# The second mixer's identity and ones move among its first constants, and its state sums move to other PSUM banks

## The chip, the core and the metric

The kernel runs on one core of a Trainium2 chip. The metric is the time of one execution on the device in microseconds (us); lower is better. A core has a matrix engine (TensorE, PE in the profile, with its weight loads as PEld), a vector engine (VectorE, DVE), a scalar engine (ScalarE, ACT), a general engine (GpSimd, POOL) and an engine that in this kernel issues nearly all transfers (SyncE, SP). Each engine runs its instructions in order and waits for semaphores that other engines or transfers raise.

## The reference, cut to what matters

One layer of a hybrid decoder runs for a prompt of 2048 tokens and for a sample group of 8 sequences with 8 tokens each (64 tokens), with the same weights:

```python
proj = x @ w_in                      # columns of mixers A, B and C
oa, delta_new = gated_delta_chunked(...)          # mixer A, chunks of 64
ob, lru_new   = rg_lru(...)                       # mixer B
oc, gla_new   = gla_chunked(qc, kc, vc, logf, s0) # mixer C, 6 heads, dk=32, dv=64
oc = head_rms_norm(oc, norm_c_w) * jax.nn.silu(zc)
heads = concatenate([oa, ob, oc])
x = layer_norm(ALPHA * x + heads @ w_out, ln1_g, ln1_b)
x = layer_norm(ALPHA * x + conv_ffn(x), ln2_g, ln2_b)
```

Mixer C in one chunk, with state S per sequence and head, and decay f = exp(logf):

```python
b = cumsum(logf); b_last = b[-1]
o     = (q * exp(b)) @ S + (att(q, k, b)) @ v
S_new = exp(b_last) * S + (k * exp(b_last - b)).T @ v
```

The prompt starts from S = 0; the sample group starts from 8 given states (s_gla), and its 8 new states are outputs.

## The kernel before

The program has four parts in a row. `phase1` makes the combined projection. `window_a` runs mixer A (`deltanet`), with a projection of the gates (`gates`) as dense filling. `window_c` runs mixer C (`Gla`) together with the output projection and the first LayerNorm (`Project`). `phase3` is the FFN; its order is written by hand. In `window_a` and `window_c` the order of the instructions on every engine, the SP queue included, is worked out when the program is built, by a planner that simulates the time line with estimated costs; program order counts as priority, and a block under `high_priority` with a negative number comes later than that.

Memory: a pool of tiles lies behind the pool made before it, and a window's pools take the addresses of the window before. A tile can be written as soon as the last reader of what lay there is done. In `window_c` the pools are, in this order: ce and cf (early tiles), c1 and c2, then those of `Project` (o1, o2, o3 with the LayerNorm rows l1g and l1b), and last c3, with the identity and the ones. The early pools lie where mixer A's early tiles were, c3 at the end, where mixer A's last working tiles were.

Mixer C works on nine groups: the sample group (number 8) first, then eight groups of 256 prompt tokens. `load` fetches b (cumulated decay), k, q and v; v has one buffer. `prep` of a group is `natural` (decay factors, on DVE and ACT), `tokens` and, for each of six heads, `fill` (builds the score operands on ACT, POOL and by transfers K<-KN) and `scores` (matmuls s, L1373). `tokens` transposes v (pv, L1394) and the decayed k (pk, L1399) on PE against the identity and copies the results on ACT into XC (L1395) and KC (L1400); for the sample group these are XCs and KCs. RC, XC and KC are rings of two for the prompt's groups.

`sample` loads the 8 states into four spare tiles of the projection (spmx, spmh, spml, spxt; two states each, L1446), makes the outputs (po, L1451 and L1453), normalizes them, and after a `yield` makes the new states: a masked copy of v (L1458), the old state times its decay (L1460), and for each of the 8 states six matmuls into a PSUM bank (ss, L1466), added on DVE (L1467) and stored (L1468). That second half is resumed when group 0 has been prepared. `chain` takes a group's four chunks in turn: new state (cs, L1427), output (po, L1430), copy of the state (L1436), and after two chunks the norm (`head_norm`).

`Project.weights` loads the eight pieces of w_out (wos, 512 KB each, through three buffers that the residual rows x share) and splits each into a high part on ACT (woh, L1495) and a low part on DVE or POOL (wol, L1496). `Project.__call__`, at low priority, multiplies 128 tokens by them (pm, L320, two tiles of 48 matmuls in all), adds the residual (L1531) and normalizes; `transposed` turns the result for the FFN (pt, L1549).

PSUM: eight banks of 2 KB per partition. Mixer C's scores have two (tag s), the transpositions one (tk), po two, cs one; the projection's pool has two (tag pm). The eight sums ss use the tag cs.

`head_norm` ends mixer A too: its last output is stored (s_mix<-ob, L986), and then the tiles it used are free.

Of the kernel before, what the change touches and what calls it, by code (L numbers as in the profile page):

```python
# [8 lines left out]
F32 = mybir.dt.float32  # L9
# [294 lines left out]
def load_consts(E, pool, names):  # L304
    t = {}
    for n in names:
        o, w = _CST[n]
        t[n] = pool.tile([128, w], F32, name="c_" + n)
        E.nc.sync.dma_start(t[n], E.d["consts"][:, o:o + w])
    return t  # L310
# [397 lines left out]
def deltanet(E, ctx, pools, need, ahead):  # L708
# [341 lines left out]
    for gs in pairs:  # L1050
        for g in gs:
            prep(g)
        inverse(gs)
        ahead(gs[0].pair)
        for g in gs:
            blocks(g)
        last = gs[-1].smp
        for g in (gs[0], *gs[2:], gs[1]):
            tokens(g)
            weights(g)  # L1060
            if g.b == 7:
                with tc.high_priority(-100):
                    sample()
            if not g.smp:
                chain(g)
# [147 lines left out]
class Gla:  # L1213
# [4 lines left out]
    def __init__(self, E, ctx):  # L1218
        nc, tc = E.nc, E.tc
        self.E = E  # L1220
        E.aset(LNEXP)
        early = ctx.enter_context(tc.tile_pool(name="ce", bufs=1))
        self.early = ctx.enter_context(tc.tile_pool(name="cf", bufs=2))
        pool = ctx.enter_context(tc.tile_pool(name="c1", bufs=1))
        self.tr = ctx.enter_context(tc.tile_pool(name="c2", bufs=2))
        self.pg = {t: ctx.enter_context(tc.tile_pool(name="c" + t, bufs=1, space=PSUM)) for t in ("s", "tk", "g")}
        self.C = load_consts(E, early, ["m2", "m3", "m2s", "bj", "i32"])

        def ring(name, n, c, w):
            return [pool.tile([128, 6, c, w], F32, name=f"{name}{i}") for i in range(n)]  # L1230

        self.RC, self.XC, self.KC = ring("RC", 2, 4, 64), ring("XC", 2, 4, 64), ring("KC", 2, 4, 32)
        sg = [early.tile([128, 6, 1, 64], F32, name="RCs")], ring("XCs", 1, 1, 64), ring("KCs", 1, 1, 32)
        self.slots = [{n: early.tile([128, 256], F32, name=f"{n}_{i}") for n in ("K1", "Q1", "K2", "Q2", "K3", "Q3")}
                      for i in range(2)]
        self.sls = [{n: early.tile([128, 64], F32, name=f"{n}_s{i}") for n in ("K2", "Q2")} for i in range(2)]

        self.KN = [{l: early.tile([128, 512 >> t], F32, name=f"KN{l}_{t}") for l in (1, 2, 3)} for t in range(2)]

        self.DD = [{l: early.tile([128, n, 6], F32, name=f"D{l}_{i}") for l, n in ((1, 4), (2, 16), (3, 64))}  # L1240
                   for i in range(2)]
        self.ebs = pool.tile([32, 6, 8], F32, name="ebs")
        for r in sg:
            nc.vector.memset(r[0][0:64], 0.0)
        nc.vector.memset(sg[0][0][64:], 0.0)
        for d in self.sls + self.KN + self.slots:
            for w in d.values():
                nc.gpsimd.memset(w, 0.0)
        for d in self.DD:
            for w in d.values():  # L1250
                nc.gpsimd.memset(w, 1.0)
        for w in self.RC + self.XC + self.KC:
            nc.gpsimd.memset(w[0:64], 0.0)
        self.G = []
        for g in range(9):
            o = Env()
            o.g, o.smp, o.t0 = g, g == 8, g * 256
            o.RC, o.XC, o.KC = (r[0] for r in sg) if o.smp else (r[g % 2] for r in (self.RC, self.XC, self.KC))
            o.nch = 1 if o.smp else 4
            o.n = 64 * o.nch  # L1260
            self.G.append(o)
# [177 lines left out]
            if c % 2 == 1:  # L1439
                self.norm(po, z, g.t0 + 64 * (c - 1))  # L1440

    def sample(self, g, room):
        nc, E, C = self.E.nc, self.E, self.C
        S0 = big = room
        for i in range(4):
            nc.sync.dma_start(S0[i][0:32], E.d["s_gla"][:, 2 * i:2 * i + 2])  # L1446
        po, z = self.outputs(g.t0)
        for h in range(6):
            p, h2 = divmod(h, 2)
            o = po[h2 * 64:(h2 + 1) * 64, p]  # L1450
            nc.tensor.matmul(o, g.XC[64:, h, 0], g.RC[64:, h, 0], start=True, stop=False)  # L1451
            for b in range(8):
                nc.tensor.matmul(o[:, b * 8:(b + 1) * 8], S0[b // 2][0:32, b % 2, h],  # L1453
                                 g.RC[0:32, h, 0, b * 8:(b + 1) * 8], start=False, stop=b == 7)
        self.norm(po, z, g.t0)
        yield
        for i in range(4):
            nc.vector.tensor_tensor(big[i][64:], g.XC[64:, None, :, 0].to_broadcast([64, 2, 6, 64]),  # L1458
                                    C["bj"][64:, 2 * i:2 * i + 2, None, None].to_broadcast([64, 2, 6, 64]), op=OP.mult)
            nc.vector.tensor_tensor(S0[i][0:32], S0[i][0:32],  # L1460
                                    self.ebs[:, :, 2 * i:2 * i + 2, None].rearrange("p h b o -> p b h o")
                                    .to_broadcast([32, 2, 6, 64]), op=OP.mult)
            for b in range(2):
                ps = self.psum(f"ss{i}{b}", (32, 6, 64), "cs", 1)
                for h in range(6):
                    nc.tensor.matmul(ps[:, h], g.KC[64:, h, 0], big[i][64:, b, h], start=True, stop=True)  # L1466
                nc.vector.tensor_tensor(S0[i][0:32, b], S0[i][0:32, b], ps, op=OP.add)  # L1467
            nc.sync.dma_start(E.d["o_glas"][:, 2 * i:2 * i + 2], S0[i][0:32])  # L1468
        yield
# [85 lines left out]
def window_c(E):  # L1555

    with ExitStack() as ctx:
        C = Gla(E, ctx)
        P = Project(E, ctx)
        C.C.update(load_consts(E, ctx.enter_context(E.tc.tile_pool(name="c3", bufs=1)), ["ident", "ones"]))  # L1560
        room = P.spare()
        C.dest = P.dest
        order = [C.G[8]] + C.G[:8]
        C.load(order[0])
        for i, g in enumerate(order):
            if i < 8:
                C.load(order[i + 1])
            C.prep(g)
            if g.smp:
                smp = C.sample(g, room)  # L1570
                next(smp)
                P.weights()
            else:
                if g.g == 0:
                    next(smp)
                C.chain(g)
            for t0 in range(g.t0, g.t0 + g.n, 128):
                with E.tc.high_priority(-10 ** 5):
                    P(t0)
                    P.transposed(C.C["ident"], 1)  # L1580
        P.transposed(C.C["ident"])
# [373 lines left out]
def program(tc, dram):  # L1955

    E = Env()
    E.nc, E.tc, E.d = tc.nc, tc, dram
    with ExitStack() as ctx:
        setup(E, ctx)  # L1960
        phase1(E)
        window_a(E)
        window_c(E)
        phase3(E)
# [16 lines left out]
```

## Time and profile before

| | us |
|---|---|
| median of 3 runs | 3026.18 |
| lowest and highest | 3017.28, 3026.94 |
| the profiled execution | 3025.96 |
| its span, first to last instruction | 3024.2 |
| PE busy in the span | 2886.8 |
| DVE, ACT, POOL busy | 1510.9, 1231.4, 844.2 |

Mixer A and the gates run from about 540 to 1037 us of the span, mixer C and the output projection from about 982 to 1525, and the FFN behind that. Times in the rows are us from the start of the span, mean times in ns where the column says so. A row of a stretch gives its bounds, its length, and then for PE, PEld, DVE, ACT and POOL the busy time and, in brackets, the number of instructions; behind them stand the granted clock of PE (1.00 is full), the share of the DMA engines and GB/s. Where a stretch is asked for one line only, only engines that run this line are shown. In a row of a line or tile the three numbers are least, median and greatest duration in ns, and then come the starts of the first and the last instruction. A row of waits reads: who waited, for whom, us in total, times, longest.

### The profile page before, as it was taken

The numbers are of one execution on the slowest core, as the hardware profiler recorded it, in microseconds if no ns is written. First come the engines' busy times: TensorE is split into PE (matmuls) and PEld (weight loads), VectorE is DVE, ScalarE is ACT, GpSimd is POOL, SyncE is SP. The second block draws the span as 40 slices with busy tenths as digits, with TensorE's granted clock in tenths as the row PEclk, the third lists the DMA queues.
The fourth block names the chain that finished last, engine by engine and source line by source line (L and its number), as shares of the span: only waits on it lengthen the run. The fifth ranks groups of instructions, "written<-read, shape, count | busy, mean of one in ns | idle before, by whom it ended". The sixth has DMA issues, their size and how long they took to land.

```text
span 3024.2 us, 45238 instructions
## 1 busy us (share of the span) xinstructions
PE 2886.8 (95%) x17755; PEld 2490.4 (82%) x17755; DVE 1510.9 (50%) x2454; ACT 1231.4 (41%) x2591; POOL 844.2 (28%) x898
## 2 busy tenths in 40 slices
PE   8999999788889799999899999999999999999998
PEld 7888789777779577767678888888889999999997
DVE  4564443577663676756533333333376443344436
ACT  4474443446653687766332222222232222222223
POOL 0000001734423545444222222222232222222224
PEclk9999999789999579999899999999999999999999
DMA  6221113533433443533531111111134111111111
GB/s 198 83 74 68 58 59 96 144 101 111 114 95 99 108 130 110 150 112 117 180 116 45 46 56 49 51 48 42 49 112 146 42 52 47 48 42 42 49 43 62
DMA packets 196508, 256.77 MB, mean 85 GB/s; under 512 B 43170, under 2 KB 162040, under 8 KB 196232
## 3 DMA queue, kind: packets, MB, share of 16 engines
q1 hardware_dynamic: 194168, 246.58, 26.6%
q0 software_dynamic: 1984, 7.12, 0.6%
q8 instruction: 140, 2.29, 0.3%
q14 instruction: 72, 0.59, 0.1%
q10 hardware_dynamic: 144, 0.20, 0.0%
HBM read 183.94 MB, written 60.08 MB: 81 GB/s over the span
## 4 chain that ended last, share of the span: by engine, by line
PE 60%; DVE 4%; ACT 2%; DMA 1%; issue 1%; POOL 1%; SPq 0%; DVEq 0%; POOLq 0%; ACTq 0%
PE pug L320 16%; PE pd L320 15%; PE puv L320 15%; PE pm L320 6%; PE s L1373 2%; DVE y L1788 1%; PE pd L1870 1%; PE cs L1427 1%; ACT Q L1360 1%; PE zp L1121 1%; PE po L1206 0%; PE zp L1122 0%; PE po L1430 0%; PE zp L1123 0%; DVE act L1724 0%
## 5 line engine op out<-in xcount | busy, mean ns | idle before, releaser
L1724 DVE SCALAR_TENSOR_TENSOR act<-G,cols,act 128x1024 f32<-128x1024 f32 (+1 forms) x132 | 123.6, 950 | 492.0 <-ACT act L1722 489.6
L1877 DVE TENSOR_TENSOR y<-y,pd 128x512 f32<-128x512 f32 x322 | 220.9, 687 | 203.2 <-PE pd L320 196.7
L1615 POOL TENSOR_TENSOR wl_d<-ws_d,wh_d 128x1024 fp32r<-128x1024 f32 x44 | 106.2, 2414 | 569.9 <-ACT wh_d L1614 523.1
L320 PE MATMUL pd<-wh_d,hh 128*128 128x512 f32 x704 | 215.4, 391 | 5.6 <-DVE y L1877 3.7
L320 PE MATMUL pd<-wh_d,hl 128*128 128x512 f32 x704 | 214.9, 390 | 0.0
L320 PE MATMUL pd<-wl_d,hh 128*128 128x512 f32 x704 | 214.6, 390 | 0.0
L1704 ACT COPY G<-pug 128x512 f32<-128x512 f32 (+2 forms) x110 | 55.0, 501 | 388.2 <-PE pug L320 388.2
L320 PE MATMUL pug<-fxh,wh_g 128*128 128x512 f32 (+2 forms) x880 | 198.0, 354 | 3.3 <-ACT wh_g L1614 2.6
L320 PE MATMUL puv<-fxh,wh_v 128*128 128x512 f32 (+2 forms) x880 | 196.4, 352 | 0.8 <-ACT wh_v L1614 0.8
L320 PE MATMUL puv<-fxh,wl_v 128*128 128x512 f32 (+2 forms) x880 | 196.2, 352 | 0.2 <-POOL wl_v L1615 0.2
L320 PE MATMUL puv<-fxl,wh_v 128*128 128x512 f32 (+2 forms) x880 | 196.0, 351 | 0.0
L320 PE MATMUL pug<-fxl,wh_g 128*128 128x512 f32 (+2 forms) x880 | 196.0, 351 | 0.0
L320 PE MATMUL pug<-fxh,wl_g 128*128 128x512 f32 (+2 forms) x880 | 195.9, 351 | 0.0
L320 PE MATMUL pm<-xh,wh 128*128 128x448 f32 (+1 forms) x800 | 181.9, 360 | 7.1 <-ACT xh L370 6.3
L1614 ACT CAST wh_d<-ws_d 128x1024 fp32r<-128x1024 f32 x44 | 45.8, 1040 | 337.5 <-PE pd L1870 173.3
L320 PE MATMUL pm<-xh,wl 128*128 128x448 f32 (+1 forms) x800 | 181.6, 359 | 0.0
L320 PE MATMUL pm<-xl,wh 128*128 128x448 f32 (+1 forms) x800 | 179.8, 358 | 0.5 <-DVE xl L371 0.4
L1766 DVE TENSOR_TENSOR hl<-act,hh 128x512 fp32r<-128x512 f32 (+2 forms) x110 | 124.0, 1128 | 99.5 <-ACT hh L1758 99.5
L320 PEld LDWEIGHTS pug<-fxh,wh_g 128*128 128x128 f32 x880 | 157.0, 189 | 19.0 <-ACT wh_g L1614 3.0
L320 PEld LDWEIGHTS puv<-fxh,wh_v 128*128 128x128 f32 x880 | 156.0, 188 | 14.9 <-ACT wh_v L1614 1.2
L320 PEld LDWEIGHTS pm<-xh,wh 128*128 128x128 f32 x800 | 144.4, 188 | 28.5 <-issue 10.1
L320 PEld LDWEIGHTS puv<-fxh,wl_v 128*128 128x128 f32 x880 | 155.6, 188 | 14.3 <-POOL wl_v L1615 0.6
(731 smaller groups left out, 6273.9 us busy)
## 6 DMA issues: line engine op xcount, KB each, us to landing
ws_d<-in_w_dn SPq DMA_DIRECT2D x44, 512.0 KB
ws_g<-in_w_up SPq DMA_DIRECT2D x43, 512.0 KB
ws_v<-in_w_up SPq DMA_DIRECT2D x43, 512.0 KB
zx<-in_xT SPq DMA_DIRECT2D x56, 256.0 KB
ws<-in_w_in SPq DMA_DIRECT2D x19, 512.0 KB
K<-KN SPq DMA_DIRECT2D x288, 32.0 KB
x<-in_x SPq DMA_DIRECT2D x16, 512.0 KB
s_x<-x SPq DMA_DIRECT2D x16, 512.0 KB
```

The costliest lines, as they stand in the source:

```text
L320: nc.tensor.matmul(ps, w[k], x[k], start=first and i == 0, stop=last and i == 3 * n - 1)
L1121: nc.tensor.matmul(ps, wh[:, k], xl, start=k == 0, stop=False)
L1360: nc.scalar.copy(v4(Q3[32 * a:32 * a + 32], 1)[:, :, a], v4(qq, 1)[:, :, a])
L1373: nc.tensor.matmul(ps[64:, c], K[:, i], Q[:, i], start=True, stop=True)
L1427: nc.tensor.matmul(ps[:, h], g.KC[:, h, c], g.XC[:, h, c], start=True, stop=True)
L1614: nc.scalar.copy(h, t)
L1615: nc.gpsimd.tensor_tensor(lo, t, h.bitcast(F32), op=OP.subtract)
L1704: nc.scalar.copy(G[:, 2 + o:2 + o + m], p[:, :m])
L1724: nc.vector.scalar_tensor_tensor(dst(act), src(i), taps[i], dst(act), op0=OP.mult, op1=OP.add)
L1766: nc.vector.tensor_tensor(dst, act[:, c], hh[:, c].bitcast(F32), op=OP.subtract)
L1788: nc.vector.scalar_tensor_tensor(y[:m, js], y[:m, js], mv[:m, tt, i:i + 1], a[:m, js], op0=op, op1=OP.add if i else OP.mult)
L1877: nc.vector.tensor_tensor(y, y, ps, op=OP.add)
```

## The change

The identity and the ones are loaded with the other constants of mixer C, into pool ce, and pool c3 goes. The eight sums of the sample group take their PSUM tile from the projection's pool (two banks, tag pm) and no longer from the bank cs.

```diff
@@ class Gla, __init__
-        self.C = load_consts(E, early, ["m2", "m3", "m2s", "bj", "i32"])
+        self.C = load_consts(E, early, ["m2", "m3", "m2s", "bj", "i32", "ident", "ones"])
...
-    def sample(self, g, room):
+    def sample(self, g, room, sums):
...
             for b in range(2):
-                ps = self.psum(f"ss{i}{b}", (32, 6, 64), "cs", 1)
+                ps = sums.tile([32, 6, 64], F32, tag="pm", name=f"ss{i}{b}")
...
@@ def window_c
         C = Gla(E, ctx)
         P = Project(E, ctx)
-        C.C.update(load_consts(E, ctx.enter_context(E.tc.tile_pool(name="c3", bufs=1)), ["ident", "ones"]))
         room = P.spare()
...
-                smp = C.sample(g, room)
+                smp = C.sample(g, room, P.pm)
```

## The prediction

> **What bounds the kernel now.** I read the page's busy line first, then busy time by stage, then the chain of waits around the place that the diff touches.
>
> ```profile
> span 3024.2 us, 45238 instructions
> PE 2886.8 (95%) x17755; PEld 2490.4 (82%) x17755; DVE 1510.9 (50%) x2454; ACT 1231.4 (41%) x2591; POOL 844.2 (28%) x898
> ```
>
> TensorE (PE) is busy for 95% of the span, so only stretches in which it idles or runs slowly can be shortened by work that is none of its own. The stages, in us: PE, weight loads, DVE, ACT, POOL, then the granted clock.
>
> ```profile
> 990.00:1040.00 50.00, 38.53 (x232) 24.30 (x231) 37.99 (x106) 41.11 (x155) 32.28 (x64) 0.57 0.33 81
> 1040.00:1046.00 6.00, 0.88 (x7) 0.52 (x5) 2.01 (x6) 1.29 (x4) 2.11 (x5) 0.50 0.78 225
> 1046.00:1061.00 15.00, 14.65 (x113) 12.93 (x112) 9.73 (x13) 4.04 (x9) 3.12 (x1) 0.50 0.59 176
> 1061.00:1083.00 22.00, 21.55 (x155) 17.00 (x155) 18.16 (x40) 20.08 (x57) 9.67 (x14) 0.50 0.62 190
> 1083.00:1106.00 23.00, 22.41 (x152) 17.33 (x152) 14.27 (x29) 14.39 (x42) 9.47 (x15) 0.87 0.49 138
> 1106.00:1165.00 59.00, 49.26 (x510) 38.21 (x508) 44.66 (x87) 52.66 (x150) 37.85 (x60) 0.96 0.32 87
> 1530.00:3024.00 1494.00, 1479.75 (x7374) 1309.90 (x7372) 629.59 (x842) 378.38 (x598) 376.17 (x218) 1.00 0.18 60
> ```
>
> The last row is the FFN: PE full at full clock, and nothing of it is touched. The change lives in the hand-over from mixer A to mixer C. There PE idles 11.5 us of 990 to 1040, 5.1 of the next 6, is full but at half clock up to 1083, and idles 9.7 us again between 1106 and 1165. The chain of waits (start, us, what) tells why all engines stop at 1040:
>
> ```profile
> 1035.15 2.04 DMA s_mix<-ob
> 1037.65 0.42 SPq L1191
> 1038.12 7.44 DMA c_ident<-in_consts
> 1045.70 0.41 PE pv L1394
> 1046.86 0.40 PE po L1451 x2
> ```
>
> Mixer A's last output store frees the memory in which pool c3 lies; SP then issues the LayerNorm rows (L1191), and the identity behind them; it is 7.44 us on its way, behind the 1 MB of those rows. The first transposition of mixer C starts 0.1 us after it lands. The rows' size, and the first load of the sample's state:
>
> ```profile
> l1g<-in_lnp SPq DMA_DIRECT2D x1, 512.0 KB
> l1b<-in_lnp SPq DMA_DIRECT2D x1, 512.0 KB
> ```
>
> ```profile
> 1039.34 0.61 SPq L1446 DMA_DIRECT2D spmx<-in_s_gla  x1
> ```
>
> Who waits in 1040 to 1062 (total us, times, longest):
>
> ```profile
> DVE spmx L1458 <- ACT XCs L1395: 8.8, 1, 8.8
> PEld pv L1394 <- DMA spmh<-in_s_gla: 5.3, 1, 5.3
> PE pv L1394 <- DMA c_ident<-in_consts: 5.1, 1, 5.1
> ```
>
> The second row is the one to keep in mind. The sample's state (in_s_gla) lands at the same moment as the identity.
>
> **The change, part by part.**
>
> (a) *Two loads move.* The constants of pool ce and the identity now:
>
> ```profile
> L309 SPq DMA_DIRECT2D c_ident<-in_consts x2: 422/426/430, 532.8 to 1038.1; - x2
> L309 SPq DMA_DIRECT2D c_i<-in_consts x2: 430/430/430, 533.8 to 911.0; - x2
> 987.17 0.54 SPq L1277 DMA_DIRECT2D v<-s_cv  x1
> ```
>
> c_i is the last constant of ce, issued at 911.0. Identity and ones will follow it there: two more SP issues of about 0.43 us, 0.9 us together, ahead of a store of mixer A. That store and the loads behind it are waited for by mixer A's engines; I cost them at nothing because PE has its gate projection to run there; without that cover they cost 0.9 us. At 1038 two issues leave SP's queue, so the state loads behind them are issued some 1.2 us earlier (1038.12 to 1039.34, the pair standing between). The block of matmuls on the state (L1451, L1453; 1046.86 to 1061) therefore starts earlier by at least nothing (if one slow DMA queue, not the issue, sets the landing) and at most 2.4 us (1046.86 less 1044.5, the landing at 1045.7 moved by the issue time). I take 1.2.
>
> (b) *Transpositions leave the crowded stretch.* v of the sample group is issued at 987.17, so the five transpositions of that group can run from about 992 on, and group 0's can follow, since v and kd have single buffers that the sample's transpositions hold. What they take of PE in the crowded stretch (first pv of L1394, then pk of L1399):
>
> ```profile
> 1040.00:1061.00 21.00, 1.24 (x3) 0.39 (x3) 0.50 0.64 190
> 1061.00:1088.00 27.00, 3.19 (x12) 1.61 (x12) 0.50 0.60 182
> 1040.00:1061.00 21.00, 0.73 (x2) 0.25 (x2) 0.50 0.64 190
> 1061.00:1088.00 27.00, 1.69 (x8) 0.93 (x8) 0.50 0.60 182
> ```
>
> 1.24 + 3.19 + 0.73 + 1.69 = 6.85 us, in a stretch where PE has 14.65 of 15 and 21.55 of 22 us busy. They go where 11.5 us of 50 are idle. Ends: 0 (PE waits there all the same, for weights or for the norm) and 6.9. I take 6.9, the nearest row being a full PE. What is late next is the state landing at 1045.7, so the idle 5 us before it need not disappear: the gain is work taken out behind it, not the gap itself. With them go the four DVE masks L1458 (they wait 8.8 us for XCs, and then need only the spare buffers).
>
> (c) *The sums take other banks.* The sample's eight state sums use the single bank cs, which the prompt's chain uses too:
>
> ```profile
> L1466 PE MATMUL ss<-spmx,KCs x24: 310/311/313, 1062.9 to 1072.9; 64*32 64x64 f32 x24
> L1466 PE MATMUL ss<-spxt,KCs x24: 215/216/240, 1101.9 to 1104.7; 64*32 64x64 f32 x24
> L1427 PE MATMUL cs<-XC,KC x384: 218/219/312, 1106.5 to 1390.6; 128*32 128x64 f32 x192
> PEld cs L1427 <- DVE spxt L1467: 0.6, 1, 0.6
> ```
>
> They run one at a time from 1062.9 to 1104.7, and the prompt's first cs starts at 1106.5, released by the last sum's addition. With the projection's two banks, two sums can be under way, and the chain of group 0 waits only for its own tiles. The chain frees RC, XC and KC for group 2 and feeds the first prompt projection, so the 9.7 us that PE idles in 1106 to 1165 (ACT at 52.66 of 59) have a cause there. Ends: 0 and 9.7. No row separates the shares, so I take half, 4.9. Matmuls, additions and stores are the same in number: 0.
>
> (d) *What is paid.* More of mixer C is ready while mixer A's last norms still run. PE has room; ACT less (41.11 of 50). The copies behind the transpositions (L1395, then L1400):
>
> ```profile
> 1040.00:1088.00 48.00, 2.50 (x6) 0.50 0.62 186
> 1040.00:1088.00 48.00, 1.40 (x4) 0.50 0.62 186
> ```
>
> 3.9 us of ACT move into a stretch with 8.9 us to spare, but each can stand ahead of one of the steps of mixer A's tail, whose store frees the memory for the state loads. Cost between 0 and 3.9; I take 1.0, because there is more room than work.
>
> (e) *Memory and order.* Pool ce grows by the 1 KB per partition that c3 gives up: the pools behind it shift, the total stays. The shift could put a tile on memory freed later; the pools it moves are first written at 982 or later, so 0. The order on all engines in mixer C is worked out by a planner, and is worked out anew: nothing in this trace prices that, and it widens the range.
>
> Sum: -1.2 - 6.9 - 4.9 + 1.0 = -12.0 us. The profiled execution took 3025.96 us (1.8 beside its span), 0.2 under the median 3026.18 of the three runs: 3025.96 - 12 = 3014. Change and no change can be told apart from about 0.3%, 9 us.
>
> **The clock, row and rule.** The stretch is slow also because of its clock:
>
> ```profile
> 985.00:990.00 5.00, 5.00 (x74) 4.65 (x72) 1.52 (x10) 4.71 (x24) 4.88 (x7) 1.00 0.33 86
> 990.00:995.00 5.00, 5.00 (x46) 4.72 (x44) 4.52 (x23) 4.80 (x25) 2.72 (x9) 0.50 0.29 79
> 1075.00:1080.00 5.00, 5.00 (x44) 4.32 (x42) 4.19 (x10) 4.82 (x15) 2.39 (x5) 0.50 0.43 108
> 1083.41 5.49 PE L320 MATMUL pm<-woh,mh 128*128 128x512 f32 x12 [0.53 <-ACT mh L1524]
> 1065.47 1.11 PE L1373 MATMUL s<-Q,K 128*64 128x64 f32 x8
> 1090.23 0.68 PE L1373 MATMUL s<-Q,K 128*64 128x64 f32 x8
> ```
>
> It falls to 0.50 at 990 with PE busy all the time, stays there through 1075 to 1080, busy again, and rises only after dense 512-column matmuls at 1083.41. The same scores take 1.11 us before and 0.68 after. So I expect the clock to follow the first dense projection, and give closing the gap no clock gain of its own. The Trainium skill ("TensorE: Matmul & The Clock Gate", Part 1) says that the full clock returns after about 3.4 us of sustained activity; the busy rows at 0.50 speak against that for these small matmuls. By it, keeping PE fed would run the whole stretch at full clock.
>
> **Rivals.**
> 1. *Hidden anyway.* The state still lands at 1045.7, and the first projection still waits for the weight pieces:
>
> ```profile
> L1495 ACT CAST woh<-wos x8: 1027/1045/1047, 1051.1 to 1088.5; 128x1024 fp32r<-128x1024 f32 x8
> ```
>
> The eighth piece is cast at 1088.5, paced by three shared buffers, and nothing in the diff loads them sooner. Then the transpositions' 6.9 us turn into waiting and only some of the rest stays: about -3 us, 3023. For it: the casts end after the projection starts at 1083.41. Against: they wait behind the very ACT and DVE work that moves away.
> 2. *The clock comes back early.* With PE fed through 1046 to 1083, 37 us of work at half clock would shrink by 1 - 0.68/1.11 = 0.39, 14 us: 3014 - 14 = 3000. For it: small matmuls ran at full clock in 985 to 990. Against: the rows at 0.50.
> 3. *Slower: the sums hold the projection's banks.* If the order still puts sums as late as now, the sample's projection, which needs both banks, starts after the last sum (1106) and not at 1083.4: 22.6 us later, with the first dense work and the clock behind it. -12 + 22.6 = about +11: 3037. It decides if the third sum pair comes after 1083. For it: half the sums do now. Against: what made them late was the single bank and the work ahead of them.
>
> **How the numbers follow.** Forecast 0.50, rival 1 0.28, rival 2 0.10, rival 3 0.12. The forecast's own ends: all small, -1.2 -6.9 -4.9 replaced by 0 with 3.9 paid gives 3030; all large, 2.4 + 6.9 + 9.7, gives 3007. Reaching towards rivals 2 and 3, and for the new order, the range is 3002 to 3031. Faster by over 0.3% is below 3017: 0.36 of the forecast's 0.50, 0.10 of rival 2, 0.04 of rival 1: 0.50. Slower: rival 3 and 0.02 of the rest: 0.14. Same: 0.36.
>
> **What would show it.** c_ident issued near 911 and the first pv before 1000 (a, b); no wait of PE for c_ident; the state block starting near 1045.5; sums ending before 1083, the first cs before 1090 (c); s_mix<-ob's last store no later than 1036 (d); the clock back before 1085. I am wrong if the last store slips by several us, if weights still end at 1088, or if sums and projection alternate on their banks.

## The result, and the profile after

| | kernel before | changed kernel |
|---|---|---|
| median, us | 3024.05 | 3053.39 |
| second measurement, in the first group of experiments, us | 3023.37 | 3050.97 |
| ratio to before, with its interval | 1 | 1.0088 [1.0069, 1.0106], again 1.0085 [1.007, 1.01] |

The change makes the kernel some 26 to 28 us slower; forecast were 12 us less. One of the first four executions of the changed kernel took 3249.96 us at a mean granted clock of 0.822 and it is the one that was profiled, so the rows here are those of a second profile (label e1, 3046.21 us, clock 0.956), and the median of the other three is 3052.21 us. Its busy line, against 2886.8 us of PE before:

```profile
span 3044.3 us, 45224 instructions
PE 2888.7 (95%) x17755; PEld 2489.9 (82%) x17755; DVE 1501.9 (49%) x2454; ACT 1232.0 (40%) x2591; POOL 854.1 (28%) x898
```

PE does the same work in 1.9 us more; the span grew by 20.1 us. So idle time was added, not work. Where? First the stretches of the prediction, then one that it did not look at (bounds, length, then PE, PEld, DVE, ACT, POOL, clock, DMA share, GB/s):

```profile
990.00:1040.00 50.00, 43.75 (x254) 27.44 (x255) 36.06 (x102) 43.11 (x163) 30.58 (x56) 0.56 0.36 94
1040.00:1046.00 6.00, 2.84 (x34) 2.14 (x32) 5.91 (x12) 5.71 (x19) 4.81 (x10) 0.93 0.75 236
1046.00:1061.00 15.00, 14.68 (x116) 13.15 (x117) 5.40 (x15) 6.11 (x14) 3.05 (x2) 0.50 0.83 197
1061.00:1083.00 22.00, 19.00 (x158) 15.53 (x158) 19.41 (x36) 17.62 (x46) 13.64 (x18) 0.66 0.45 135
1106.00:1165.00 59.00, 54.56 (x507) 43.62 (x507) 48.34 (x103) 43.77 (x128) 32.42 (x52) 1.00 0.42 116
1165.00:1310.00 145.00, 137.84 (x1079) 107.12 (x1078) 97.21 (x202) 101.92 (x307) 67.05 (x119) 0.95 0.42 123
1455.00:1530.00 75.00, 43.16 (x183) 30.36 (x183) 29.73 (x31) 20.01 (x33) 21.78 (x14) 0.75 0.49 156
```

The last stretch is the hand-over from the output projection to the FFN. The kernel before, there and in the stretch ahead of it:

```profile
1165.00:1310.00 145.00, 142.21 (x1109) 111.66 (x1108) 102.31 (x203) 100.09 (x299) 63.49 (x116) 0.99 0.45 133
1455.00:1530.00 75.00, 61.29 (x259) 46.76 (x260) 35.41 (x37) 27.87 (x44) 25.84 (x17) 0.86 0.52 166
```

PE loses 61.29 - 43.16 = 18.1 us there, at the far end from the edit. The waits in 1440 to 1530 name it (who, for whom, us, times, longest), in the changed kernel:

```profile
POOL fxl L1665 <- PE pt L1549: 22.8, 1, 22.8
PE pug L320 <- ACT fxh L1666: 18.5, 2, 14.3
```

L1665 is the load of the FFN's input, from x1T (L1666 in the kernel before; lines after the diff are one less). The POOL queue waits 22.8 us for the last transposition of the output projection, which reads the identity, and the FFN's first matmuls (pug) wait for the pieces behind that load. The load is only a part of that wait. It lands 5.4 us after its issue (median of the five), but ACT casts the pieces only at 1509.3: it stands at the copies of the last transpositions, which wait for the store before them (s_x1T) to land:

```profile
1508.34 1.07 ACT L1550 COPY xt<-pt 128x512 f32<-128x512 f32 x2 [15.53 <-DMA s_x1T<-xt]
1509.30 2.00 ACT L1666 CAST fxh<-fxl 128x1024 fp32r<-128x1024 f32 x2
```

In the kernel before, the five pieces loaded on POOL were cast ahead of the copies of the last transpositions, from 1471.7 on. Starts of these loads and of the transpositions, before and then changed (first and last start):

```profile
L1666 POOL DMA_DIRECT2D fxl<-s_x1T x5: 538/554/563, 1466.8 to 1477.7; - x5
L1549 PE MATMUL pt<-c_ident,x x136: 270/273/445, 1155.4 to 1507.1; 128*128 128x128 f32 x136
```

```profile
L1665 POOL DMA_DIRECT2D fxl<-s_x1T x5: 540/557/563, 1496.4 to 1514.9; - x5
L1549 PE MATMUL pt<-c_ident,x x136: 270/272/476, 1140.7 to 1495.7; 128*128 128x128 f32 x136
```

Before, the loads are issued 40.3 us ahead of the last transposition; now 0.7 us behind it, though that transposition comes 11.4 us sooner. In c3 the identity lay at the end of the window's memory; pool ce is at its start, and the FFN's first input tiles go there. Moving the load also moved the place that the last reader holds. The experiments test whether that place is what the loads wait for.

### The profile page after: what moved, and what is told of

Its sections match the earlier page's. It is cut to its first block, busy times and chain, and to the rows that moved or that the text cites. A ratio compares the mean times of both kernels' runs of the same rounds, so it can differ in the third digit from the quotient of the medians.

```text
span 3248.1 us, 45224 instructions
## 1 busy us (share of the span) xinstructions
PE 3109.5 (96%) x17755; PEld 2582.1 (79%) x17755; DVE 1499.9 (46%) x2454; ACT 1232.4 (38%) x2591; POOL 847.8 (26%) x898
## 4 chain that ended last, share of the span: by engine, by line
PE 50%; issue 1%; DVE 0%; POOL 0%; POOLq 0%; DVEq 0%
PE puv L320 16%; PE pug L320 16%; PE pd L320 16%; PE pd L1869 1%; DVE fxl L1667 0%; DVE y L1876 0%; POOL wl_g L1614 0%; DVE y L1837 0%; DVE y L1838 0%; DVE l2st L1941 0%; DVE y L1811 0%; DVE y L1810 0%; DVE l2mv L1826 0%; DVE l2sh L1779 0%; POOLq L1614 0%
## 5 line engine op out<-in xcount | busy, mean ns | idle before, releaser
L320 PE MATMUL pd<-wh_d,hh 128*128 128x512 f32 x704 | 232.2, 416 | 1.7 <-DVE y L1876 1.7
L320 PE MATMUL pug<-fxh,wh_g 128*128 128x512 f32 (+2 forms) x880 | 214.2, 375 | 19.9 <-ACT fxh L1666 17.8
L320 PE MATMUL pd<-wl_d,hh 128*128 128x512 f32 x704 | 232.7, 417 | 0.0
L320 PE MATMUL pd<-wh_d,hl 128*128 128x512 f32 x704 | 232.4, 417 | 0.0
L320 PE MATMUL pug<-fxl,wh_g 128*128 128x512 f32 (+2 forms) x880 | 214.1, 375 | 1.9 <-POOL fxl L1667 1.8
L320 PE MATMUL pug<-fxh,wl_g 128*128 128x512 f32 (+2 forms) x880 | 213.7, 375 | 0.2 <-POOL wl_g L1614 0.2
L320 PE MATMUL puv<-fxl,wh_v 128*128 128x512 f32 (+2 forms) x880 | 212.0, 373 | 0.0
L1613 ACT CAST wh_d<-ws_d 128x1024 fp32r<-128x1024 f32 x44 | 45.7, 1040 | 375.3 <-PE pd L1869 191.5
L320 PEld LDWEIGHTS pug<-fxl,wh_g 128*128 128x128 f32 x880 | 163.4, 193 | 26.1 <-POOL fxl L1667 3.2
L320 PEld LDWEIGHTS pug<-fxh,wl_g 128*128 128x128 f32 x880 | 163.5, 193 | 21.7 <-POOL wl_g L1614 0.7
L320 PEld LDWEIGHTS puv<-fxl,wh_v 128*128 128x128 f32 x880 | 162.6, 192 | 21.1
```

The lines of the kernel that those rows point to most:

```text
L320: nc.tensor.matmul(ps, w[k], x[k], start=first and i == 0, stop=last and i == 3 * n - 1)
L1613: nc.scalar.copy(h, t)
```

## The experiments

e5, e6 and e8 are the kernel before with the edit named, all others the changed one. The kernel before ran beside each group: 3023.37 us (e1 to e4), 3024.75 (e5 to e8), 3023.96 (e9 to e11) and 3024.50 (e12). To tell stretches apart I read five marks off the rows of each profile: mixer A's first and last output store, the last matmul of the projection on two high parts (pm<-woh,mh), the last x1T load on SP (of the FFN's second block, in the middle of the FFN), and the end. Before, the four stretches between them are 346.6, 454.2, 718.3 and 816.5 us. I call the third one the hand-over. Each row of marks is one execution.

| kernel | median | ratio to before | last store | store to last pm | pm to last x1T load |
|---|---|---|---|---|---|
| before (profile) | | 1 | 1035.2 | 454.2 | 718.3 |
| e1: changed | 3050.97 | 1.0085 [1.007, 1.01] | 1038.9 | 447.5 | 742.8 |
| e2: identity only | 3056.42 | 1.0103 [1.0088, 1.0118] | 1042.8 | 457.2 | 742.6 |
| e3: sums only | 3026.19 | 1.0011 [1.0001, 1.0021] | 1039.8 | 454.8 | 718.5 |
| e4: identity behind c2 | 3038.88 | 1.005 [1.0034, 1.0065] | 1041.6 | 455.1 | 729.0 |
| e5: place only (as meant) | 3052.46 | 1.0091 [1.0071, 1.011] | 1038.8 | 452.0 | 744.5 |
| e6: resident identity, no sums | 3036.07 | 1.0037 [1.0022, 1.0052] | 1041.8 | 456.2 | 718.9 |
| e7: resident identity and sums | 3026.78 | 1.0009 [0.9998, 1.002] | 1042.8 | 454.4 | 719.2 |
| e8: mixer A's memory freed sooner | 3034.43 | 1.0025 [1.001, 1.0041] | 1041.0 | 457.8 | 720.1 |
| e9: FFN tiles moved by 512 bytes | 3048.88 | 1.0083 [1.0071, 1.0096] | 1039.8 | 447.4 | 743.6 |
| e10: e9, weights first | 3046.68 | 1.0077 [1.0064, 1.0089] | 1039.7 | 444.9 | 744.9 |
| e11: e9, transpositions later | 3051.07 | 1.0097 [1.0083, 1.0111] | 1041.4 | 450.4 | 744.0 |
| e12: identity in its own pool | 3028.14 | 1.0012 [1.0003, 1.0021] | 1042.0 | 449.2 | 718.8 |

**e1, the changed kernel again; e2 and e3, one part each.** e2 puts `ss` back on the tag cs; e3 puts the identity and the ones back into c3.

> The changed kernel as it is, for a second profile. Three theories of the loss. Lifetime: the identity now lies where the FFN's first input piece goes and is read by the last transposition pt, so the loads of that piece wait for it; expects about 3051 us, the first x1T load (POOL queue) after the last pt, and some 20 us more PE idle at the start of the FFN than the 13.7 us idle in 1455 to 1530 of before. Crowding: mixer C's work, now ready early, delays mixer A's last store; expects the same time, but the last store 10 us or more later against its first store than the 346.6 us of before. Banks: the state sums and the projection wait for each other; expects PE waits of pm or ss for DVE additions of 10 us or more in sum.

> Only the identity and ones move into pool ce; the sums stay in bank cs. Lifetime: the whole loss or nearly so, 3043 to 3055 us. Crowding: also the whole loss. Banks: no loss, 3015 to 3028 us.

> Only the sums move to the projection's banks; identity and ones stay in pool c3 at the end. Lifetime and crowding: no loss, 3015 to 3028 us. Banks: the loss, 3040 to 3055 us.

Measured: in e1 the last store comes 3.7 us later after the first than before, not 10; e2 carries the loss (hand-over 742.6), e3 none of it (718.5). The sums alone cost some 3 us (0.3 to 6.3 by the interval).

**e4, the identity early, but at another place** (its pool c3 made right behind c2):

```diff
+        mid = ctx.enter_context(tc.tile_pool(name="c3", bufs=1))
...
-        self.C = load_consts(E, early, ["m2", "m3", "m2s", "bj", "i32", "ident", "ones"])
+        self.C = load_consts(E, early, ["m2", "m3", "m2s", "bj", "i32"])
+        self.C.update(load_consts(E, mid, ["ident", "ones"]))
```

> The change, but with identity and ones in a pool behind c2, memory that mixer A's gates free at about 982 us and that the FFN fills last, beside the output weights that it must wait for anyway. Lifetime: the loss is gone, 3010 to 3028 us, the first x1T load issued before the last pt. Crowding: identity is there by about 986, all the work of mixer C is ready as early as in the change, so the loss stays, 3040 to 3055 us. Banks: the loss stays too.

```profile
L1667 SPq DMA_DIRECT2D fxl<-s_x1T x11: 320/424/570, 1510.1 to 2225.7; - x11
L1667 POOL DMA_DIRECT2D fxl<-s_x1T x5: 538/554/561, 1474.2 to 1485.1; - x5
```

The five loads on POOL are free again, and now the three on SP come late: at 1510.1, 0.3 us behind the last transposition (1509.8), against 1493.4 before. These go into the pool fx1, which lies further up. The wait moved with the place: 10.7 us of hand-over remain of 24.5. Neither forecast held: 3038.88 us lies between the two, since the new place is under FFN tiles as well.

**e5, the place alone.** The tiles lie in ce; their load was to be held back to where it was before, by a small copy that waits for a tile in c3, and the sums stay on cs:

```diff
+        hold = ctx.enter_context(E.tc.tile_pool(name="c3", bufs=1)).tile([128, 1], F32, name="hold")
+        E.nc.vector.memset(hold, 0.0)
+        for n, t in C.held.items():
+            E.nc.vector.tensor_copy(t[:, 0:1], hold)
...
```

> Identity and ones lie in pool ce as in the change, but are loaded as late as before (their load waits for a tile of pool c3's place), and the sums stay in bank cs. So the place is changed and the time of arrival is not. Lifetime: the loss of the FFN's start alone, 3043 to 3052 us; from the last high-part projection matmul to the second load of x1T 740 us or more, against 718.3 before. Crowding: no loss, 3018 to 3030 us, since mixer C has its identity no sooner than before.

```profile
L1562 DVE MEMSET hold<- x1: 59/59/59, 235.5 to 235.5; 128x1 f32 x1
L1566 SPq DMA_DIRECT2D c_ident<-in_consts x1: 1397/1397/1397, 912.2 to 912.2; - x1
POOL fxl L1673 <- PE pt L1550: 23.1, 1, 23.1
```

The load was not held back. The tile in c3 was written at 235.5 us already, so the identity was loaded at 912.2 and not at 1038.1, and its first transposition (pv) runs at 1001.4. e5 is therefore e2 once more, with the same loss (1.0091, hand-over 744.5), and does not part the place from the time of arrival. The next two do.

**e6 and e7, one identity for both mixers**, in a pool made before `window_a` and kept to the end, so that it lies under no FFN tile; e6 without the sums, e7 with them:

```diff
+        E.fp = ctx.enter_context(tc.tile_pool(name="fix", bufs=1))
...
+    E.fix = load_consts(E, E.fp, ["ident", "ones"])
```

> One identity and one ones tile, loaded for mixer A, in a pool of their own that stays to the end of the program; mixer C loads none, and the sums stay in bank cs. So mixer C has its identity early and the FFN's tiles do not lie on it. Lifetime: no loss at the FFN's start (718 us between the same two marks), 3010 to 3028 us. Crowding: mixer C's work still crowds mixer A's tail, last store 6 us or more later than 1035.2, 3032 to 3042 us.

> The same with the sums on the projection's banks: both aims of the change without its place in memory. Lifetime: 718 us between the marks; with the 3 us by which mixer C ended sooner in the second profile of the change, 3015 to 3025 us; my prediction's 3014 if its gain was there at all. Crowding: 3030 us or more.

Both have the old hand-over (718.9, 719.2), though the identity is loaded at 507.5 (e6) and 507.8 (e7) and the first transpositions run at 1004.6 (e6) and 1004.9 (e7), some 40 us sooner than the 1045.7 of before. So the early identity is not what costs at the hand-over, but the place of a tile that is read to the end. What is left is what the change is worth without its place, as far as these two show it: e6 is 1.0037, e7 1.0009 of before. With the early identity alone, e6 is 11 us slower, as the crowding theory forecast for it; with it, the sums' own banks bring 9 us back (5 between e2 and e1). Neither is a gain. Where e6's 11 us arise is not shown: in its profile the last store is 6.6 us later and the way to the last pm 2.0 longer, but most of the 6.6 was there before any of the moved work (see (d) below).

**e8, the place of c3 freed sooner** (mixer A's kv tiles moved to a last pool of their own; the identity back in c3):

> Before, but mixer A's pool of k and v tiles lies last, so the place of pool c3 is free when mixer A's last transposition is done, and identity and ones can land early without a move; sums in bank cs. Lifetime: no loss at the FFN's start, 3010 to 3030 us. Crowding: as for the resident identity, 3032 to 3042 us. The order of mixer A's first loads changes too, which can be some us either way.

It gives about what e6 gives (1.0025, last store 1041.0), by another way to an early identity (loaded at 959.7). That speaks for the early work as the cause of these some 10 us, and not for the place; it does not show it.

**e9, e10, e11: the FFN's tiles moved off the identity.** e9 puts the identity first in ce and an unused tile of the same 512 bytes first in the FFN's memory; e10 adds the weights ahead of the sample's outputs, e11 a lower priority for the first transpositions:

```diff
+        ident = early.tile([128, 128], F32, name="c_ident")
...
+        pad = ctx.enter_context(tc.tile_pool(name="fpad", bufs=1)).tile([128, 128], F32, name="pad")
         xp = [ctx.enter_context(tc.tile_pool(name="fx0", bufs=1))]
```

> The changed kernel whole: identity and ones among the first constants and the sums on the projection's banks. Only addresses differ: the identity lies first in pool ce, and the FFN begins with an unused tile of 512 bytes per partition, so that its first input pieces no longer lie on the identity; every order and every instruction is as in the changed kernel. Lifetime: the FFN's first x1T loads no longer wait for the last transposition; the POOL queue issues them near 1475, before the last transposition and not after it as at 1496.4; the stretch from the last dense projection tile to the second block's loads falls from 742.8 to about 719 us, and the time by about 24 us, from 3051 to about 3027, which is no difference from the kernel before. Crowding: the loss lies in mixer C, the time stays at 3045 to 3052, and the stretch near 743.

> As e9, and the weights of the output projection come before the outputs of the sample group in program order, and so in the planner's priority: weight pieces are fetched and split before the state block. If the weights pace the first dense projection, the last piece is split before 1085, the first dense tile starts some 5 us earlier than in e9, and the time is 3 to 8 us below that of e9, about 3021; if only the work behind matters, the state's block moves later into the full stretch, and the time is that of e9 or some us above it.

> As e9, and the transpositions of the sample group and of group 0 come at a lower priority than the scores, so that a few scores go ahead of them on PE and ACT while mixer A ends. If the early transpositions are what delays mixer A's last store (1038.9 against 1035.2 in the kernel before), the store comes back to about 1036 and the time is some 3 us below that of e9; otherwise the store stays at 1038 or later, and the time at that of e9.

My theory missed here: no input tile of the FFN lies on the identity any more, and nothing is gained.

```profile
POOL fxl L1670 <- PE pt L1553: 24.7, 1, 24.7
```

The wait is the same. Two readings were left: a wait counts for whole pools (the input tiles still lie on the rest of ce), or the identity's earlier load changes an order. In e10 the last weight piece is cast at 1077.3 (1091.4 in e9), as was wanted, but the first pm starts later, not sooner (1088.7 against 1083.0), and the time is only some 2 us under that of e9; e11's last store comes at 1041.4, not back at 1036. So the gain that each was to show did not come: neither the weights' priority nor the transpositions' alone sets these ends.

**e12, the bound between two pools.** Addresses of identity and FFN tiles as in e9; the identity has its own pool ahead of ce:

```diff
-        ident = early.tile([128, 128], F32, name="c_ident")
+        ident = ctx.enter_context(tc.tile_pool(name="ci", bufs=1)).tile([128, 128], F32, name="c_ident")
         early = ctx.enter_context(tc.tile_pool(name="ce", bufs=1))
```

> As e9 (the changed kernel, with an unused tile of 512 bytes ahead of the FFN's input tiles), but the identity has a pool of its own ahead of ce, so that the unused tile lies exactly on that pool, and the input tiles begin where ce begins. Addresses of the identity and the FFN's tiles are those of e9; what differs is the bound between two pools. Lifetime by whole pools: a tile waits for every reader of a pool that its own pool overlaps, which would be why e9 did not help; now the first loads need only the last norm, the POOL queue issues them near 1475, the stretch from the last dense tile to the second block's loads falls from 743.6 to about 719 us, and the time from 3049 to about 3026. If the wait hangs on something else that the early identity brings (its place among the loads, the order that the planner makes), nothing changes against e9: first load after the last transposition near 1498, 3049 us.

The rows of its loads and transpositions, and the stretch of the hand-over:

```profile
L1670 POOL DMA_DIRECT2D fxl<-s_x1T x5: 537/554/561, 1468.8 to 1479.7; - x5
L1553 PE MATMUL pt<-c_ident,x x136: 270/273/448, 1140.9 to 1509.0; 128*128 128x128 f32 x136
```

```profile
1455.00:1530.00 75.00, 59.56 (x266) 45.67 (x265) 35.07 (x37) 27.89 (x43) 22.76 (x16) 0.89 0.51 164
```

The loads go out 40.2 us before the last transposition, PE is busy 59.56 us again, and the time falls by 20.7 us to 3028.14. One more thing differs from e9: the identity is loaded at 825.8 instead of 915.7. That speaks against the second reading all the more, as the load is earlier still and the wait is gone. So in this program a tile waits for every reader of every pool that its own pool overlaps, not of the bytes it takes; the description of the kernel before, by which a tile can be written when the last reader of what lay there is done, is too narrow. In fact the tile that the first load fills never lay on the identity: a high part of 4352 bytes lies ahead of it, and the seven constants at the start of ce have 3488 (sums of the tiles' sizes in the code); it lies on working tiles further back in ce. That settles the cause of the loss at the hand-over: the identity, as a part of ce, holds the FFN's whole first pool until the output projection has transposed its last rows. No kernel tried beats the one before; e3, e7 and e12 come within some 0.1%.

## Why the prediction was wrong, point by point

**(e) Memory and order, costed at 0: the step that failed.** It asked when the pools are first written, which was right for mixer A's side. It did not ask until when they are read, and what the FFN puts there; the sentence that nothing of the FFN is touched rests on the same gap. Missed term: +24.5 us (742.8 - 718.3). The rows needed were in the trace of before: loads of x1T from 1466.8, and an identity read until 1507.1. An identity placed under those loads could hold them by up to 40 us, more than all that was to be saved.

**(a) Loads, -1.2.** The constants were issued near 915, as forecast, without harm that mixer A's next stores show (1.3 us late at 912.9, ahead of them, and 1.4 at 963.1):

```profile
L309 SPq DMA_DIRECT2D c_ident<-in_consts x2: 430/478/526, 532.0 to 915.2; - x2
L1446 SPq DMA_DIRECT2D spmx<-in_s_gla x1: 420/420/420, 1041.8 to 1041.8; - x1
```

From mixer A's last store to the first state load it is 3.0 us instead of 4.2, so the forecast 1.2 is there. But that store slipped by 3.7 (see (d)): the load went out at 1041.8 and not sooner than 1039.3, and the last matmul on the state ends at 1063.6 instead of 1061.1, 2.5 us later.

**(b) Transpositions, -6.9.** They left: the first pv starts at 1000.2, PE is busy 43.75 us of 990 to 1040 (38.53 before), and no wait of PE for c_ident is left. What came in their place are the transpositions of the next group (first L1394, then L1399):

```profile
1040.00:1061.00 21.00, 1.69 (x8) 0.90 (x8) 0.62 0.80 208
1061.00:1088.00 27.00, 2.13 (x8) 1.08 (x8) 0.72 0.48 140
```

```profile
1061.00:1088.00 27.00, 1.26 (x8) 0.75 (x8) 0.72 0.48 140
```

1.69 + 2.13 + 1.26 = 5.08 us, of 6.85 before: 1.8 us net. And the first projection hardly moved with them: 1082.1 against 1083.4. It follows the cast of its own input, the sample group's outputs (mh). That cast, before and then in the changed kernel:

```profile
L1524 ACT CAST mh<-mx x1: 1027/1027/1027, 1082.3 to 1082.3; 128x1024 fp32r<-128x1024 f32 x1
L1524 ACT CAST mh<-mx x1: 1028/1028/1028, 1080.8 to 1080.8; 128x1024 fp32r<-128x1024 f32 x1
```

Those outputs need the state, which came no sooner. Rival 1 named the state and the weight pieces. The pieces are cast as late as before, but they did not set this start: in e10 all are cast by 1078.4, mh at 1084.1, and the projection starts at 1088.7. Inside the projection PE waits 1.6 us for a piece. The casts in the changed kernel, the waits around them in 1046 to 1106, and last the same wait for the transfers before:

```profile
L1495 ACT CAST woh<-wos x8: 1032/1045/1046, 1053.5 to 1090.4; 128x1024 fp32r<-128x1024 f32 x8
```

```profile
ACT woh L1495 <- DMA wos<-in_w_out: 8.2, 4, 3.7
POOL wol L1496 <- ACT woh L1495: 10.2, 1, 10.2
```

```profile
ACT woh L1495 <- DMA wos<-in_w_out: 0.5, 1, 0.5
```

That the casts waited "behind the very ACT and DVE work that moves away" was the wrong argument: with it gone, ACT waits 8.2 us for the transfers instead of 0.5.

**(c) Sums, -4.9.** The sums did not end before 1083; they came after the projection:

```profile
L1466 PE MATMUL ss<-spmx,KCs x24: 216/216/240, 1106.8 to 1108.8; 64*32 64x64 f32 x24
L1466 PE MATMUL ss<-spxt,KCs x24: 216/216/240, 1122.0 to 1124.4; 64*32 64x64 f32 x24
L1427 PE MATMUL cs<-XC,KC x384: 219/219/316, 1039.2 to 1396.2; 128*32 128x64 f32 x192
```

The last sum is issued at 1124.4, where it was 1104.7. This is rival 3's lateness without its price, since the planner let the projection have the banks first. The chain of group 0 did come free: first cs at 1039.2 instead of 1106.5. PE's idle time in 1106 to 1165 fell from 9.74 to 4.44 us, 5.3 us gained where 4.9 was forecast. The banks did it: e3, with the sums alone, idles 2.2 us there, and e2, without them, 10.8. That the size came out so near was luck, since half of 9.7 had been taken for want of a row. And in 1165 to 1310 idle time rose from 2.79 to 7.16, so that 4.4 of it was gone; e2 idles 9.6 us there too, without a gain ahead of it, and e3 10.5, so the cause of this rise stays open.

**(d) Mixer A's tail, +1.0.** The last store came at 1038.9 against 1035.2: +3.7, in the upper part of the bounds 0 to 3.9. But not all of that is the early work. Starts of mixer A's stores:

| kernel | twelfth of 17 | third from last | second from last | last |
|---|---|---|---|---|
| before | 911.6 | 1010.3 | 1022.1 | 1035.2 |
| e1: changed | 912.9 | 1011.4 | 1026.1 | 1038.9 |
| e3: sums only | 916.4 | 1014.7 | 1026.4 | 1039.8 |
| e6: resident identity, no sums | 916.6 | 1013.9 | 1029.1 | 1041.8 |
| e12: identity in its own pool | 915.4 | 1014.5 | 1029.1 | 1042.0 |

In e3 the identity is loaded at 1042.7, so nothing of mixer C is early by it, and yet the last store is 4.6 us late; all of that was there at the twelfth store, some 70 us before mixer C begins. So a few us of delay in a single profile need not come from the change. What goes with the early identity is the step from the third-last to the second-last store: 11.8 us before and 11.7 in e3, but some 15 in e1, e6 and e12. The cost is thus near 3 us where 1.0 was taken: the direction was right, the size not. Which of the early instructions delays it stays open, as e11 did not bring it back.

**The sum.** Mixer C with its projection took 447.5 us from the last store to the last pm, 6.7 less than before; with the tail's 3.7 the gain is 3.0 us (1489.4 to 1486.4), where 12.0 was forecast and rival 1 said 3. That rival 1's number came out is luck in part, as the weight pieces did not hold the start of the projection. Then come +24.5 at the hand-over and -1.4 behind it, which makes the span's +20.1. None of the rivals named this place. The stated range, 3002 to 3031, also left out the times of its own rivals 2 and 3 (3000 and 3037), which had 0.22 of the chances.

**The clock.** Closing the gap did not bring it back for the stretch, as forecast: it is 0.50 in 1046 to 1061 with PE busy 14.68 of 15 us. But it did not wait for the first dense projection (1082.1) either, as was forecast too: it is 0.93 in 1040 to 1046 and 0.66 in 1061 to 1083, where it was 0.50 before. The rule of the Trainium skill ("TensorE: Matmul & The Clock Gate", Part 1), full clock after some 3.4 us of sustained activity, does not describe 1046 to 1061, if PE's busy time in the profile counts as such activity.

## What to carry to other kernels

A constant that moves to an earlier pool is held from its load to its last reader, and at its new place something else will be written: look up the last read in the trace and the first write of the next stage there, before anything is costed at nothing. Where memory is handed on by whole pools, that look-up has to take every tile of the pools that overlap, and a tile that is read to the end of a stage belongs into a pool of its own that no early pool of the next stage overlaps, or behind everything that the next stage writes first. An experiment that is to hold something back is worth a look in its own trace whether it did. And where PE is full and other engines are late too, work moved out of a crowded stretch lets the next group's work move in, so count it as gained only if the wait that ends last moves as well.

## What was not expected of the hardware

In these rows of the changed kernel the granted clock is low where PE is full of small matmuls and mostly higher where it has gaps:

```profile
1025.00:1030.00 5.00, 3.59 (x20) 2.23 (x19) 3.37 (x10) 4.78 (x18) 1.24 (x4) 0.50 0.43 107
1040.00:1042.00 2.00, 1.27 (x18) 0.99 (x16) 1.94 (x6) 1.91 (x7) 1.64 (x6) 1.00 0.39 111
1063.00:1068.00 5.00, 5.00 (x41) 4.23 (x41) 4.97 (x8) 3.18 (x9) 3.22 (x4) 0.50 0.09 24
1068.00:1073.00 5.00, 2.74 (x23) 1.88 (x22) 4.91 (x6) 3.38 (x9) 4.81 (x5) 0.84 0.44 124
1073.00:1078.00 5.00, 5.00 (x44) 4.39 (x42) 4.88 (x15) 4.38 (x12) 2.76 (x7) 0.50 0.66 232
```

2.74 us of work in 5 at a clock of 0.84, between two rows with 5.00 of 5 at 0.50. Part of it may be the reverse, that at half clock the same work fills the time; and 1025 to 1030 had 0.50 with 3.59 us busy. No experiment here took it apart.
